# TensorE's order at the stage boundaries, a written order for the first norm, and GpSimd's work as written, in a two-layer hybrid decoder

## The chip, the cores and the metric

The kernel runs on one core of a Trainium2 chip. The metric is the device time of one launch in microseconds (us). The engines that matter are TensorE (PE in the profile: matrix products and transposes, results in the eight banks of PSUM), VectorE (DVE), ScalarE (ACT), GpSimd (POOL) and SyncE (SP, which only issues transfers). Each engine works through its own queue in order, and waits by semaphores for the others.

## What is computed

Two layers over 512 tokens of width 1024 in float32, each a half-weighted SwiGLU feed-forward, four token mixers between two projections, and a second feed-forward; a last norm ends it. Cut to what the change touches:

```python
D_MODEL = 1024; SEQ = 512; DEPTH = 2; D_FF = 2816

def rmsnorm(x, g):
    xf = x.astype(jnp.float32)
    y = xf * lax.rsqrt(jnp.mean(xf * xf, axis=-1, keepdims=True) + EPS)
    return (y * g.astype(jnp.float32)).astype(x.dtype)

def swiglu(h, w1, w3, w2):
    return (jax.nn.silu(h @ w1) * (h @ w3)) @ w2

for l in range(DEPTH):
    h = rmsnorm(x, ffn1_norm[l])
    x = x + FFN_RESIDUAL * swiglu(h, ffn1_w1[l], ffn1_w3[l], ffn1_w2[l])
    h = rmsnorm(x, mix_norm[l])
    p = h @ w_in[l]
...
    mix = jnp.concatenate([y_a, y_b, y_c, y_d], axis=-1)
    x = x + mix @ w_out[l]
    h = rmsnorm(x, ffn2_norm[l])
    x = x + FFN_RESIDUAL * swiglu(h, ffn2_w1[l], ffn2_w3[l], ffn2_w2[l])
return rmsnorm(x, final_norm)
```

## The kernel before

The 512 tokens are four blocks b = 0 to 3 of 128 (tiles `x0` to `x3`, rows are tokens). Every float32 operand of a product is split into a high part (a rounded copy, made by ScalarE as a cast) and a low part (the rest, made by VectorE as a subtraction), and each product is three TensorE passes: high by high, activation low by weight high, activation high by weight low (`mm3`, lines 107 to 109). In the feed-forwards the products follow a Strassen-like scheme on halves of the tokens: r = 1 are blocks 2 and 3, r = 0 are blocks 0 and 1.

The class `Norm` makes a normed operand in steps: `square` (ScalarE, one per half row, sums into `ss`), `root` (VectorE adds to `nv`, GpSimd raises to the power -1/2 into `ry`), `scale` (VectorE, `xn`), and `turn`: TensorE transposes the block into two banks `pt` (8 transposes of 128x128), ScalarE casts the high part (L210, or L189 for the mixers), VectorE subtracts the low part (L211, L190), and for the feed-forwards ScalarE also keeps plain copies (`B12f`, `B22f`, L214 and L215). `B12` and `B22` are the operands of blocks 2 and 3, `B11` and `B21` those of blocks 0 and 1; `third` makes one more operand, T3, from the plain copies.

There are four feed-forwards, named f0a, f0b, f1a, f1b (layer, then a for the one ahead of the mixers and b for the one behind), each `up` and then `down`; the mixers are L0 and L1, their norms m0 and m1. `up` begins with the last pair of columns without the scheme: 192 matmuls of 128x256, 96 for r = 1, then the transposes of blocks 0 and 1 (`turns`), then 96 for r = 0, all in the order of `mm3`. Its weights come in four quarters (m, k), each a transfer, a cast `whi` and a subtraction `wlo`. The mixers end with the output projection: eight banks `po` (block b, half c), to each of which `part(b, c)` adds 18 matmuls of 128x512 and, when the last mixer's result `ya` is there, the final loop 6 more; then VectorE adds the bank to x (L847), and the next norm begins.

TensorE's order is the written one (`manual_schedule` for PE). Inside `down` VectorE and ScalarE are also in written order; elsewhere a scheduler with priorities orders VectorE, ScalarE, GpSimd and the transfers. GpSimd also issues transfers that add to a tile (`accum_op`), lines 333, 336 and 393. The program opens with 40 matmuls on a constant (`WARM`), and the first norm, n0.

Of the kernel before, what the change touches and what calls it, by code (L numbers as in the profile page):

```python
# [42 lines left out]
C_ALL = C_R16 + 32  # L43
# [6 lines left out]
def trunk(ctx: ExitStack, tc: tile.TileContext, x, par, gains, tab, w13, w2, wi, wg, wo, out):  # L50
    nc = tc.nc
# [191 lines left out]

    HALF = (slice(0, 256), slice(256, 512))

    def up(f, nrm, turns, name):
        a = [
            [acts.tile([P, n, T], F32, tag=f"a{h}{j}", name=f"a{h}{j}_{name}") for j, (_, n) in enumerate(SUB)]  # L250
            for h in range(2)
# [13 lines left out]
        W = (P, 2, 4, P)

        def quarters(i):
            return {
                (m, k): load(w13[f, i, m, k], W, f"{name}{i}{m}{k}") for m in range(2) for k in range(2)
            }  # L270
# [313 lines left out]
    def mixers(l, nrm, nxt, turns):  # L584
# [89 lines left out]
        mix = {}  # L674
# [155 lines left out]
            mix[j] = split2(y, f"ya_{nm}{j}")  # L830


        wa = []
        for c in range(2):
            raw = load(wo[l, c, :, 6:8], (P, 2, T), f"{nm}oa{c}")
            wa.append(split_w(raw, (P, 2, T), f"{nm}oa{c}", acts, (f"q{2 * c}", f"q{2 * c + 1}")))
        part(0, 1)
        part(1, 1)
        for b in (2, 3, 0, 1):
            bs = slice(b * P, (b + 1) * P)  # L840
            for c in range(2):
                for e in range(2):
                    hi, lo = mix[e]
                    mm3(pw[b, c], hi[:, bs], lo[:, bs], wa[c][0][:, e], wa[c][1][:, e], False, e == 1)
                with tc.high_priority(offset=400):
                    xs = xt[b][:, c * T : (c + 1) * T]
                    V.tensor_tensor(xs, pw[b, c], xs, ALU.add)  # L847
                nxt.square(b, c)
            nxt.scale(b)
        for b in (2, 3):  # L850
            nxt.turn(b)


    ctx.enter_context(tc.manual_schedule(engines={mybir.EngineType.PE}))

    pd = bank("pd")
    for i in range(WARM):
        PE.matmul(pd[:, 0:P], mean_w, mean_w, start=True, stop=True)
    nrm = Norm("n0", 0)
    for b in (2, 3):  # L860
        for c in range(2):
            nrm.square(b, c)
        nrm.scale(b)
    for b in (0, 1):
        nc.sync.dma_start(xt[b], x[b])
# [4 lines left out]
    pt = const.tile([P, C_ALL], F32, name="pt")  # L870
    nc.sync.dma_start(pt, par)
    for b in (2, 3):
        nrm.turn(b)
    for l in range(DEPTH):

        def turns(nrm=nrm):
            for b in (0, 1):
                nrm.turn(b)

        nx = Norm(f"m{l}", 3 * l + 1)  # L880
        ffn(2 * l, nrm, nx, f"f{l}a", turns)
        nrm = nx

        def turns(nrm=nrm):
            for b in (0, 1):
# [12 lines left out]
        nrm = nx
# [84 lines left out]
```

## Time and profile before

| what | value |
|---|---|
| time, median of 3 runs | 1680.32 us (1679.66 to 1680.62) |
| the profiled execution's own time | 1681.03 us |
| its span, first to last instruction | 1679.3 us |
| PE busy | 98% of the span |
| DVE, ACT, POOL busy | 78%, 51%, 9% |
| mean granted TensorE clock | 0.993 |

TensorE is busy nearly all the time, so the table alone shows no room; what is to be read is where its few idle stretches lie, what ended each, and where the granted clock was 0.5. All times in rows are us from the start of the span, durations of single instructions in us.

### The profile page before, as it was taken

To read this page: it belongs to the slowest core of one execution; us is meant where nothing else is said; L and a number is where in the kernel's file an instruction comes from. 1 tells how busy PE (TensorE), PEld (TensorE's weight loads), DVE (VectorE), ACT (ScalarE), POOL (GpSimd) and SP (SyncE) were. 2 spreads that over 40 slices of the span, in tenths; PEclk is the share of its full clock that TensorE was granted. 3 is DMA by queue.
4 is the path that set the end of the run, shared out by engine and by line. 5 is a ranking of instruction groups with operands and counts; after the bars stand their busy time and mean duration, and the time that the engine had idled before them with its cause. 6 is when DMAs were issued, how large, how long until landed. Compare 5 with 4: busy or idle time off the path is not lost.

```text
span 1679.3 us, 27504 instructions
## 1 busy us (share of the span) xinstructions
PE 1645.1 (98%) x11072; PEld 1520.0 (91%) x11072; DVE 1307.3 (78%) x1661; ACT 850.0 (51%) x1238; POOL 145.5 (9%) x170
## 2 busy tenths in 40 slices
PE   8999999999998999999999999999999999999997
PEld 8999998888788999998899999988887799999886
DVE  5777778979856777788987777889796677777887
ACT  5454555553334555555655454556333445554654
POOL 1000002010010000101001000010000100000100
PEclk9999999999999999999999999999999999999999
DMA  6677669643331777779457777795333347777882
GB/s 203 189 182 182 177 195 242 190 157 101 113 87 63 183 185 182 191 204 263 151 132 184 187 182 184 200 270 182 119 90 97 90 113 178 186 180 185 234 229 101
DMA packets 80479, 283.94 MB, mean 169 GB/s; under 512 B 8928, under 2 KB 9056, under 8 KB 80352
## 3 DMA queue, kind: packets, MB, share of 16 engines
q1 hardware_dynamic: 61920, 217.18, 39.6%
q0 software_dynamic: 18432, 65.02, 22.3%
q8 instruction: 86, 1.41, 0.3%
q14 instruction: 41, 0.34, 0.1%
HBM read 280.07 MB, written 2.10 MB: 168 GB/s over the span
## 4 chain that ended last, share of the span: by engine, by line
PE 91%; DVE 5%; issue 1%; ACT 1%; POOL 1%; DMA 0%; POOLq 0%; DVEq 0%; ACTq 0%
PE px_f0b L107 3%; PE px_f1b L107 3%; PE px_f1a L107 3%; PE px_f1a L108 3%; PE px_f0a L108 3%; PE px_f0a L109 3%; PE px_f0b L109 3%; PE px_f1b L109 3%; PE px_f0a L107 3%; PE px_f1b L108 3%; PE px_f0b L108 3%; PE px_f1a L109 3%; PE pi_L L108 3%; PE pi_L L107 3%; PE pi_L L109 3%; PE pz_f1a L107 2%
## 5 line engine op out<-in xcount | busy, mean ns | idle before, releaser
L107 PE MATMUL pi_L<-gh_m,whi_L0i 128*128 128x512 f32 (+1 forms) x128 | 47.5, 371 | 0.3 <-ACT gh_m L189 0.3
L107 PE MATMUL pi_L<-gh_m,whi_L1i 128*128 128x512 f32 (+1 forms) x128 | 47.5, 371 | 0.3 <-ACT gh_m L189 0.3
L108 PE MATMUL pi_L<-gl_m,whi_L1i 128*128 128x512 f32 (+1 forms) x128 | 46.6, 364 | 0.6 <-DVE gl_m L190 0.6
L108 PE MATMUL pi_L<-gl_m,whi_L0i 128*128 128x512 f32 (+1 forms) x128 | 46.6, 364 | 0.6 <-DVE gl_m L190 0.6
L109 PE MATMUL pi_L<-gh_m,wlo_L0i 128*128 128x512 f32 (+1 forms) x128 | 46.4, 363 | 0.0
L109 PE MATMUL pi_L<-gh_m,wlo_L1i 128*128 128x512 f32 (+1 forms) x128 | 46.4, 363 | 0.0
L794 DVE SCALAR_TENSOR_TENSOR scr_gv_L<-scr_cv_L,pt,scr_gv_L 128x511 f32<-128x511 f32 (+29 forms) x60 | 43.8, 731 | 0.6
L794 DVE SCALAR_TENSOR_TENSOR scr_cv_L<-scr_cv_L,pt,scr_cv_L 128x511 f32<-128x511 f32 (+29 forms) x60 | 43.7, 728 | 0.1
L107 PEld LDWEIGHTS pi_L<-gh_m,whi_L0i 128*128 128x128 f32 x128 | 24.2, 189 | 4.9 <-ACT gh_m L189 0.6
L108 PEld LDWEIGHTS pi_L<-gl_m,whi_L1i 128*128 128x128 f32 x128 | 24.2, 189 | 4.8 <-DVE gl_m L190 0.8
L107 PEld LDWEIGHTS pi_L<-gh_m,whi_L1i 128*128 128x128 f32 x128 | 24.2, 189 | 4.8 <-ACT gh_m L189 0.6
L108 PEld LDWEIGHTS pi_L<-gl_m,whi_L0i 128*128 128x128 f32 x128 | 24.2, 189 | 4.8 <-DVE gl_m L190 0.8
L97 ACT CAST whi_L0i<-raw_L0i 128x1024 fp32r<-128x1024 f32 x14 | 14.6, 1051 | 27.4 <-PE pi_L L108 16.5
L97 ACT CAST whi_L1i<-raw_L1i 128x1024 fp32r<-128x1024 f32 x14 | 14.6, 1050 | 27.1 <-PE pi_L L108 16.2
L109 PEld LDWEIGHTS pi_L<-gh_m,wlo_L0i 128*128 128x128 f32 x128 | 24.2, 189 | 3.8
L109 PEld LDWEIGHTS pi_L<-gh_m,wlo_L1i 128*128 128x128 f32 x128 | 24.2, 189 | 3.8
L211 DVE TENSOR_TENSOR B_b<-pt_b,B_b 128x512 fp32r<-128x512 f32 x16 | 10.1, 681 | 19.7 <-ACT B_b L210 19.7
L108 PE MATMUL p_f0b<-B_b,whi_f0b 128*128 128x256 f32 x64 | 19.6, 307 | 2.8 <-DVE B_b L211 2.8
L108 PE MATMUL p_f1b<-B_b,whi_f1b 128*128 128x256 f32 x64 | 19.4, 304 | 2.8 <-DVE B_b L211 2.8
L107 PE MATMUL p_f0b<-B_b,whi_f0b 128*128 128x256 f32 x64 | 19.5, 305 | 2.2 <-ACT B_b L210 2.2
L107 PE MATMUL p_f1b<-B_b,whi_f1b 128*128 128x256 f32 x64 | 19.3, 302 | 2.2 <-ACT B_b L210 2.2
L107 PE MATMUL p_f0a<-B_n,whi_f0a 128*128 128x256 f32 x64 | 18.9, 295 | 2.1 <-ACT whi_f0a L278 1.8
(3407 smaller groups left out, 7281.5 us busy)
## 6 DMA issues: line engine op xcount, KB each, us to landing
raw_L0i<-wi SPq DMA_DIRECT2D x14, 512.0 KB, 3.7
raw_L1i<-wi SPq DMA_DIRECT2D x14, 512.0 KB, 3.7
tt_f0a<-w POOLq DMA_DIRECT2D x10, 512.0 KB, 8.5
tt_f0b<-w POOLq DMA_DIRECT2D x10, 512.0 KB, 8.6
tt_f1a<-w POOLq DMA_DIRECT2D x10, 512.0 KB, 8.7
tt_f1b<-w POOLq DMA_DIRECT2D x10, 512.0 KB, 8.3
gain<-gains SPq DMA_DIRECT2D x7, 512.0 KB, 4.5
raw_L0o<-wo SPq DMA_DIRECT2D x6, 512.0 KB, 3.8
```

The costliest lines, as they stand in the source:

```text
L97: S.copy(hi, raw)
L107: PE.matmul(ps, sh, mh, start=first, stop=False, skip_group_check=more)
L108: PE.matmul(ps, sh, ml, start=False, stop=False, skip_group_check=more)
L109: PE.matmul(ps, sl, mh, start=False, stop=last, skip_group_check=more)
L211: V.tensor_tensor(lo[:, :, s], ps[q], hi[:, :, s].bitcast(F32), ALU.subtract)
L794: V.scalar_tensor_tensor(acc[:, kk:], v[:, : T - kk], cw, acc[:, kk:], ALU.mult, ALU.add)
```

## The change

Six things change. (1) At the start 24 constant matmuls stand in place of 40, with 3 more behind each of the first two transposed blocks; the first norm's VectorE, ScalarE and SP work is in written order, in which blocks 2 and 3 are finished before blocks 0 and 1, and two of the first weight quarters are fetched ahead of `x0` and `x1`. (2) The 192 opening matmuls of `up` go by part: for each r and m all high by high (16), then all activation low (16), then all weight low (16). (3) `turns`, the transposes of blocks 0 and 1, stand 32 matmuls earlier, inside r = 1, and `third` ahead of r = 1. (4) In the mixers `turns` stands one group of 24 matmuls earlier. (5) At the end of the mixers blocks 2 and 3 are finished ahead of `part(1, 1)`, and their transposes stand between the last groups of blocks 0 and 1; the last two weight tiles share two buffers (q0, q1) in place of four (q0 to q3). (6) GpSimd's instructions stand in written order.

```diff
-WARM = 40
+WARM = 24
...
         ps = {(m, e): bank(f"p{2 * e + 1}_{name}{i}{m}") for m in range(2) for e in range(2)}
+        nrm.third()
+
         for r in (1, 0):
             for m in range(2):
-                for e in range(2):
-                    for k in range(KD):
-                        hi, lo = w[m, k // 4]
-                        g = nrm.op[f"B{k // 4 + 1}{r + 1}"]
-                        mm3(
-                            ps[m, e][:, HALF[r]], hi[:, e, k % 4], lo[:, e, k % 4],
-                            g[0][:, k % 4], g[1][:, k % 4], k == 0, k == KD - 1,
-                        )
-            if r == 1:
-                nrm.third()
-                turns()
+                for n, (x, y) in enumerate(((0, 0), (0, 1), (1, 0))):
+                    if (r, m, n) == (1, 1, 1):
+                        turns()
+                    for e in range(2):
+                        for k in range(KD):
+                            PE.matmul(
+                                ps[m, e][:, HALF[r]], w[m, k // 4][x][:, e, k % 4],
+                                nrm.op[f"B{k // 4 + 1}{r + 1}"][y][:, k % 4],
+                                start=n == 0 and k == 0, stop=n == 2 and k == KD - 1,
+                            )
...
         proj_mm(pg, wgate, HALF[1])
+        turns()
         proj_mm(pv, wval, HALF[1])
-        turns()
...
-            wa.append(split_w(raw, (P, 2, T), f"{nm}oa{c}", acts, (f"q{2 * c}", f"q{2 * c + 1}")))
+            S.copy(wah[:, c], raw)
+            V.tensor_tensor(wal[:, c], raw, wah[:, c].bitcast(F32), ALU.subtract)
+
+        def ending(b, c):
+            bs = slice(b * P, (b + 1) * P)
+            for e in range(2):
+                hi, lo = mix[e]
+                mm3(pw[b, c], hi[:, bs], lo[:, bs], wah[:, c, e], wal[:, c, e], False, e == 1)
+            with tc.high_priority(offset=400):
+                xs = xt[b][:, c * T : (c + 1) * T]
+                V.tensor_tensor(xs, pw[b, c], xs, ALU.add)
+            nxt.square(b, c)
+
         part(0, 1)
+        for b in (2, 3):
+            ending(b, 0)
+            ending(b, 1)
+            nxt.scale(b)
         part(1, 1)
-        for b in (2, 3, 0, 1):
...
+        for b in (0, 1):
+            ending(b, 0)
+            nxt.turn(2 + b)
+            ending(b, 1)
+            nxt.scale(b)
+
+
+    ctx.enter_context(tc.manual_schedule(engines={mybir.EngineType.PE, mybir.EngineType.Pool}))
...
+    with tc.manual_schedule(
+        engines={mybir.EngineType.DVE, mybir.EngineType.Activation, mybir.EngineType.SP}
+    ):
+        for k in range(2):
+            raw[0, k] = quarter_of(0, KH - 1, 0, k, "f0a")
+        for b in (0, 1):
+            nc.sync.dma_start(xt[b], x[b])
+        for k in range(2):
+            raw[1, k] = quarter_of(0, KH - 1, 1, k, "f0a")
+        pt = const.tile([P, C_ALL], F32, name="pt")
+        nc.sync.dma_start(pt, par)
+        warm_up(WARM)
+        for b in (2, 3):
             for c in range(2):
+                nrm.square(b, c)
+            nrm.scale(b)
...
         for b in (2, 3):
+            nrm.turn(b)
+            warm_up(3)
```

Where this moves instructions is seen at three places. At the start, ScalarE's queue before had all eight squares (`sq`, block and half in the name) and then the casts of blocks 2 and 3 ahead of the first weight:

```order
L136 ACTIVATE sq_n031_151,ss_n03_148<-x3_84 128x512
L136 ACTIVATE sq_n000_162,ss_n00_161<-x0_81 128x512
...
L136 ACTIVATE sq_n011_175,ss_n01_172<-x1_82 128x512
L210 CAST B12_n0_185<-pt_n020_189 128x4x128
L210 CAST B22_n0_186<-pt_n021_196 128x4x128
L210 CAST B12_n0_185<-pt_n030_205 128x4x128
L210 CAST B22_n0_186<-pt_n031_212 128x4x128
L278 CAST whi_f0a1000_241<-raw_f0a1000_233 128x1024
L278 CAST whi_f0a1001_245<-raw_f0a1001_235 128x1024
L214 COPY B12f_n0_187<-pt_n020_189 128x4x128
```

and now has, from the last square of block 3 on:

```order
L136 ACTIVATE sq_n031_149,ss_n03_146<-x3_84 128x512
L277 CAST whi_f0a1000_234<-raw_f0a1000_99 128x1024
L210 CAST B12_n0_157<-pt_n020_161 128x4x128
L210 CAST B22_n0_158<-pt_n021_168 128x4x128
L277 CAST whi_f0a1001_238<-raw_f0a1001_101 128x1024
L214 COPY B12f_n0_159<-pt_n020_161 128x4x128
L136 ACTIVATE sq_n000_201,ss_n00_200<-x0_81 128x512
L215 COPY B22f_n0_160<-pt_n021_168 128x4x128
L210 CAST B12_n0_157<-pt_n030_180 128x4x128
L136 ACTIVATE sq_n001_203,ss_n00_200<-x0_81 128x512
L210 CAST B22_n0_158<-pt_n031_187 128x4x128
L136 ACTIVATE sq_n010_212,ss_n01_211<-x1_82 128x512
```

The weight casts moved ahead of squares and copies, and block 3's two casts behind block 0's squares. At the end of the mixers of layer 0, TensorE's queue before was: the last group of block 1, all transposes of blocks 2 and 3 (`pt_b02`, `pt_b03`), and then the three passes of `up` in turn:

```order
L109 MATMUL po_L011_4800<-whi_L0oa1_4777,scr_ya_L01h_4766 128x512
L163 MATMUL pt_b020_4925<-ident_89,xn_b02_4844 128x128 x4
L163 MATMUL pt_b021_4932<-ident_89,xn_b02_4844 128x128 x4
L163 MATMUL pt_b030_4941<-ident_89,xn_b03_4869 128x128 x4
L163 MATMUL pt_b031_4948<-ident_89,xn_b03_4869 128x128 x4
L107 MATMUL p1_f0b100_4993<-B12_b0_4921,whi_f0b1000_4977 128x256
L108 MATMUL p1_f0b100_4993<-B12_b0_4921,whi_f0b1000_4977 128x256
L109 MATMUL p1_f0b100_4993<-B12_b0_4921,wlo_f0b1000_4979 128x256
```

and now block 3's transposes have a group of block 1 behind them, and `up` opens with high parts alone:

```order
L163 MATMUL pt_b030_4917<-ident_89,xn_b03_4841 128x128 x4
L163 MATMUL pt_b031_4924<-ident_89,xn_b03_4841 128x128 x4
L107 MATMUL po_L011_4843<-oah_L0_4762,scr_ya_L00h_4752 128x512
...
L109 MATMUL po_L011_4843<-oah_L0_4762,scr_ya_L01h_4759 128x512
L291 MATMUL p1_f0b100_4984<-B12_b0_4872,whi_f0b1000_4968 128x256 x4
L291 MATMUL p1_f0b100_4984<-B22_b0_4873,whi_f0b1001_4972 128x256 x4
L291 MATMUL p3_f0b100_4985<-B12_b0_4872,whi_f0b1000_4968 128x256 x4
L291 MATMUL p3_f0b100_4985<-B22_b0_4873,whi_f0b1001_4972 128x256 x4
```

On VectorE the same place before had block 3's low parts at the end, directly behind each other:

```order
L148 TENSOR_SCALAR nv_b01_4915<-ss_b01_4903 128x1
L211 TENSOR_TENSOR B12_b0_4921<-pt_b020_4925,B12_b0_4921 128x4x128
L156 SCALAR_TENSOR_TENSOR xn_b01_4919<-x1_82,ry_b01_4917,gain2_4838 128x1024
L211 TENSOR_TENSOR B12_b0_4921<-pt_b030_4941,B12_b0_4921 128x4x128
L211 TENSOR_TENSOR B22_b0_4922<-pt_b021_4932,B22_b0_4922 128x4x128
L211 TENSOR_TENSOR B22_b0_4922<-pt_b031_4948,B22_b0_4922 128x4x128
```

and now has a weight's low part (L279), three adds to x and a `scale` (L156) between them:

```order
L211 TENSOR_TENSOR B22_b0_4873<-pt_b021_4883,B22_b0_4873 128x4x128
L847 TENSOR_TENSOR x0_81<-po_L001_4772,x0_81 128x512
L279 TENSOR_TENSOR wlo_f0b1010_4978<-raw_f0b1010_4964,whi_f0b1010_4976 128x1024
L148 TENSOR_SCALAR nv_b00_4901<-ss_b00_4869 128x1
L847 TENSOR_TENSOR x1_82<-po_L010_4651,x1_82 128x512
L156 SCALAR_TENSOR_TENSOR xn_b00_4905<-x0_81,ry_b00_4903,gain2_4810 128x1024
L211 TENSOR_TENSOR B12_b0_4872<-pt_b030_4917,B12_b0_4872 128x4x128
L847 TENSOR_TENSOR x1_82<-po_L011_4843,x1_82 128x512
L211 TENSOR_TENSOR B22_b0_4873<-pt_b031_4924,B22_b0_4873 128x4x128
```

Block 2's low parts moved ahead, and block 3's behind work for blocks 0 and 1. On GpSimd four powers `ry` of the second feed-forward's norm now stand ahead of its first two adding transfers, and the mixers' mask behind the powers of their norm.

## Rows read from the trace of the kernel before

**Rows 1.** List of TensorE's waits: waited for, us in total, times, longest.
```profile
PE p_f0b L108 <- DVE B_b L211: 2.8, 2, 2.3
...
PE pi_L L108 <- DVE gl_m L190: 1.1, 2, 0.6
...
PE p_f1a L108 <- DVE B_a L211: 0.6, 1, 0.6
```

**Rows 2.** Busy time by stretch: stretch, length, five engines (instructions), granted clock, DMA.
```profile
19.03:22.45 3.42, 3.08 (x14) 3.08 (x15) 3.42 (x4) 1.56 (x3) 0.00 (x0) 0.50 0.64 164
...
507.14:513.97 6.83, 6.04 (x28) 6.04 (x29) 4.38 (x6) 2.81 (x4) 0.00 (x0) 0.50 0.22 77
1333.16:1339.99 6.83, 5.24 (x24) 5.24 (x25) 5.07 (x6) 3.13 (x5) 0.00 (x0) 0.50 0.22 77
```

**Rows 3.** Timeline of TensorE, start and f0a: start, us, instruction, idle before.
```profile
1.13 11.21 PE L858 MATMUL pd<-mean_w 128*128 128x128 f32 x80 [1.13 <-DVE expo L66]
...
19.37 0.58 PE L109 MATMUL p_f0a<-B_n,wlo_f0a 128*128 128x256 f32 x1 [1.94 <-DVE wlo_f0a L280]
...
31.85 0.28 PE L108 MATMUL p_f0a<-B_n,whi_f0a 128*128 128x256 f32 x1
31.97 0.28 PE L109 MATMUL p_f0a<-B_n,wlo_f0a 128*128 128x256 f32 x1
32.09 1.91 PE L163 MATMUL pt_n<-ident,xn_n 128*128 128x128 f32 x16
...
35.51 0.28 PE L109 MATMUL p_f0a<-B_n,wlo_f0a 128*128 128x256 f32 x1
```

**Rows 4.** Timeline of TensorE, end of mixers L0 and opening of f0b.
```profile
482.45 0.39 PE L107 MATMUL po_L<-whi_L0o,scr_yc_L00h 128*128 128x512 f32 x1
...
501.50 1.91 PE L163 MATMUL pt_b<-ident,xn_b 128*128 128x128 f32 x16
505.25 0.39 PE L107 MATMUL p_f0b<-B_b,whi_f0b 128*128 128x256 f32 x1 [1.84 <-ACT B_b L210]
507.93 0.58 PE L108 MATMUL p_f0b<-B_b,whi_f0b 128*128 128x256 f32 x1 [2.29 <-DVE B_b L211]
...
514.03 0.28 PE L109 MATMUL p_f0b<-B_b,wlo_f0b 128*128 128x256 f32 x1
```

**Rows 5.** Timeline of VectorE (first row) and ScalarE, start.
```profile
7.94 2.48 DVE L156 SCALAR_TENSOR_TENSOR xn_n<-x,ry_n,gain 128x1024 f32<-128x1024 f32 x2
...
9.17 0.63 ACT L136 ACTIVATE sq_n<-x 128x512 f32<-128x512 f32 x1 [1.58 <-DMA x<-x]
...
10.68 0.63 ACT L136 ACTIVATE sq_n<-x 128x512 f32<-128x512 f32 x1
...
16.62 1.10 ACT L214 COPY B12f_n<-pt_n 128x512 f32<-128x512 f32 x2
17.58 1.10 ACT L278 CAST whi_f0a<-raw_f0a 128x1024 fp32r<-128x1024 f32 x1
```

**Rows 6.** SP's timeline, then the second of these two issues: KB, us to landing.
```profile
2.19 0.99 SPq L865 DMA_DIRECT2D x<-x  x2
...
x<-x SPq DMA_DIRECT2D x1, 512.0 KB, 7.8
```

**Rows 7.** Timeline, end of mixers L0: VectorE, GpSimd.
```profile
483.26 0.69 DVE L713 TENSOR_TENSOR scr_ya_L01h<-scr_cv_L,scr_ya_L01h 128x512 fp32r<-128x512 f32 x1
...
507.19 1.88 DVE L211 TENSOR_TENSOR B_b<-pt_b,B_b 128x512 fp32r<-128x512 f32 x3
...
503.26 0.55 POOL L114 TENSOR_TENSOR ry_b<-nv_b,expo 128x1 f32<-128x1 f32 x1 [3.12 <-DVE nv_b L148]
```

**Rows 8.** Timeline, opening of f1a: TensorE, GpSimd.
```profile
846.67 0.28 PE L107 MATMUL p_f1a<-B_a,whi_f1a 128*128 128x256 f32 x1
...
848.95 0.39 PE L109 MATMUL p_f1a<-B_a,wlo_f1a 128*128 128x256 f32 x1 [0.44 <-DVE wlo_f1a L280]
...
854.28 1.40 POOL L114 TENSOR_TENSOR ry_a<-nv_a,expo 128x1 f32<-128x1 f32 x1 [1.59 <-DVE nv_a L148]
```

More of the change, by code (lines that the diff above doesn't have):

```diff
@@ L244, in trunk, with quarter_of, up @@
     HALF = (slice(0, 256), slice(256, 512))
-    def up(f, nrm, turns, name):
+    W = (P, 2, 4, P)
+    def quarter_of(f, i, m, k, name):
+        return load(w13[f, i, m, k], W, f"{name}{i}{m}{k}")
+    def up(f, nrm, turns, name, raw=None):
         a = [
@@ L263, in sums @@
             V.tensor_tensor(a21, a11, a21, ALU.subtract)
[L265 to L270, printed above, removed]
         i = KH - 1
-        raw = quarters(i)
+        if raw is None:
+            raw = {(m, k): quarter_of(f, i, m, k, name) for m in range(2) for k in range(2)}
         w = {}
@@ L557, in down, with ffn @@
                     nxt.scale(t)
-    def ffn(f, nrm, nxt, name, turns, end=False):
-        down(f, *up(f, nrm, turns, name), nxt, name, end)
+    def ffn(f, nrm, nxt, name, turns, end=False, raw=None):
+        down(f, *up(f, nrm, turns, name, raw), nxt, name, end)
     class Scratch:
@@ L830, in mixers @@
             mix[j] = split2(y, f"ya_{nm}{j}")
-        wa = []
+        wah, wal = (acts.tile([P, 2, 2, T], F32R, tag=f"q{e}", name=f"oa{'hl'[e]}_{nm}") for e in range(2))
         for c in range(2):
             raw = load(wo[l, c, :, 6:8], (P, 2, T), f"{nm}oa{c}")
-            wa.append(split_w(raw, (P, 2, T), f"{nm}oa{c}", acts, (f"q{2 * c}", f"q{2 * c + 1}")))
+            S.copy(wah[:, c], raw)
[9 more added lines that the diff above has]
+            nxt.square(b, c)
@@ L837, in mixers @@
         part(0, 1)
+        for b in (2, 3):
+            ending(b, 0)
+            ending(b, 1)
+            nxt.scale(b)
         part(1, 1)
-        for b in (2, 3, 0, 1):
-            bs = slice(b * P, (b + 1) * P)
-            for c in range(2):
[L842 to L849, printed above, removed]
@@ L850, in mixers @@
-        for b in (2, 3):
[L851 to L865, printed above, removed]
+        for b in (0, 1):
[3 more added lines that the diff above has]
+            nxt.scale(b)
@@ new lines, in trunk, with warm_up @@
+    ctx.enter_context(tc.manual_schedule(engines={mybir.EngineType.PE, mybir.EngineType.Pool}))
+    pd = bank("pd")
+    def warm_up(n):
+        for _ in range(n):
+            PE.matmul(pd[:, 0:P], mean_w, mean_w, start=True, stop=True)
+    nrm = Norm("n0", 0)
+    raw = {}
+    with tc.manual_schedule(
[11 more added lines that the diff above has]
+        for b in (2, 3):
+            for c in range(2):
+                nrm.square(b, c)
+            nrm.scale(b)
+        for b in (2, 3):
+            nrm.turn(b)
+            warm_up(3)
@@ L869, in trunk @@
         nrm.scale(b)
[L870 to L873, printed above, removed]
     for l in range(DEPTH):
@@ L880, in trunk @@
         nx = Norm(f"m{l}", 3 * l + 1)
-        ffn(2 * l, nrm, nx, f"f{l}a", turns)
+        ffn(2 * l, nrm, nx, f"f{l}a", turns, raw=raw)
+        raw = None
         nrm = nx
```

## The prediction

> **What bounds the kernel now.** TensorE: it is busy 98% of the span, so an edit pays only where TensorE stands idle or runs at half clock. I read the list of its waits first, then the granted clock by stretch, then the timeline of TensorE at each place the list names, and last the engines it waits for. The list names places where one stage hands over to the next: the openings of `up`, the transposes of blocks 0 and 1, the mixers' first projections [rows 1]. [...] Inside the long loops of `up` and `down` nothing is named, so nothing there is counted.
>
> Two paces are needed. At full clock a 128x256 matmul starts 0.12 behind the last (31.85, 31.97 [rows 3]); a transpose too (16 in 1.91). At half clock 14 start in 3.08, about 0.213 each [rows 2].
>
> **The transposes of blocks 0 and 1 (edits 3 and 4).** In f0a 16 transposes begin at 32.09; unhindered the third matmul behind them would start 1.79 + 3 x 0.12 later, at about 34.2. It starts at 35.51 [rows 3]: 1.35 lost, waiting for the casts and then the low parts of what was just transposed. The same wait stands in the list for f0b (2.8 in two waits of which one is 2.3), f1a (0.6) and twice for the mixers (1.1 in two) [rows 1]; f1b has the same code. Now 32 matmuls of 128x256 in `up` (3.8 us), or 24 in the mixers (2.9), lie between transposes and use. The chain to be hidden ends 1.35 late, so both cover it: 5 places (f0a is counted below) x 1.35 = 6.8 gained. The bound from the other side: with the transposes 32 matmuls earlier the normed blocks 0 and 1 must be ready earlier. In f1a TensorE now gets there at 846.67 + 64 x 0.12 = 854.35 [rows 8], while block 1's power ended at 854.28 + 1.40 = 855.7 and the `scale` needs 1.24 more [rows 5, 8]. In the new order the first power no longer stands behind an adding transfer and T3's subtraction stands behind block 0's `scale`, which I put at 1.3 earlier for the whole chain: ready at about 855.6, while block 0's 8 transposes last until 855.3. So 0.4 is lost there (none to 2).
>
> **The opening of f1a (edit 2).** TensorE waits 0.44 for `wlo`, and a lone matmul in a stopped stream costs 0.26 more (0.38 in place of 0.12) [rows 8]. The low weights are now used 32 matmuls (3.8 us) later: 0.7 gained.
>
> **The end of the mixers (edits 2 and 5), f0b and f1b.** In f0b the transposes begin at 501.50; unhindered the 30th matmul of `up` would start 1.79 + 29 x 0.12 later, at 506.8. It starts at 514.03 (28 of them within the half-clock stretch) [rows 2, 4]: 7.3 lost, some 4.8 by the two waits and 2.5 by the clock. In f1b the clock came back 0.8 earlier in the program (1339.99 against 513.97 + 826.82, the distance of the two places), so 6.9.
>
> What is late next? Take the new order with durations of before: adds to x and low parts of a transposed half block 0.63 [rows 7], a `scale` 1.24, a square 0.76, a copy or cast of a half block 0.55, a cast or low part of a weight 1.1 to 1.2 [rows 5], a power 0.55 [rows 7], a group of six 128x512 matmuls 1.36 (0.227 each: 18 from 482.45 take 4.08 [rows 4]). Three checks:
> First, the endings now begin behind `part(0, 1)`, 4.08 after 482.45, at 486.5; `ya` is complete at 483.26 + 0.69 = 483.95 [rows 4, 7], so 2.6 of slack are left of the 6.6 that were there.
> Second, block 3 must be scaled when its transposes come up, at 501.2 (486.5, four groups 5.4, `part(1, 1)` 4.1, three groups and a block of transposes 5.1). Its second square stands behind a weight cast that waits for `part(1, 1)`; I get 498.0. Slack 3.
> Third, `up` opens at 503.6 with 16 high matmuls and needs block 3's casts then (503.1 and 503.6, just in time), and block 3's low parts at 505.6 and 506.1. VectorE has in its queue, from 499.2 on: add, two low parts, add, a weight's low part, `nv`, add, `scale` (with a power ahead), low part, add, low part: 505.7 for the first, 506.95 for the second. So TensorE waits about 0.1 and then 0.85, and 0.25 to start again: 1.2, with 0.2 for one more change between transposes and matmuls 1.4 (0 if VectorE keeps up; 3 if a power or a cast is late). Nothing there leaves TensorE idle as long as the 1.84 and 2.29 of before, so the clock should stay up. Gained: 7.3 + 6.9 - 2 x 1.4 = 11.4.
>
> **The start (edit 1).** `x2`, `x3` and the gain keep their places in SP's queue, so the first `scale` still starts at 7.94 [rows 5]. The new order puts block 3's `nv` behind it: second `scale` 10.1 to 11.4. Warm-up matmuls end at about 8.6 (48 of the 80 passes; the first 20 run at 0.21, by the time of before [rows 3]), block 2's transposes follow at 9.3, block 3's at 11.4 to 12.3, the last warm-ups end at 13.0. The first weight quarter takes `x0`'s place and lands at 9.1, which is when the square waiting for `x0` starts [rows 5]; the second takes `x1`'s, 2.67 + 7.8 = 10.4 [rows 6]; `x0` and `x1` come 1.3 apart behind, 11.7 and 13.0. ScalarE then runs, from 9.15: weight cast, two casts, weight cast, copy, square, copy, cast (ends 14.9), square, cast (ends 16.1). TensorE starts four matmuls at 14.9 and streams from 16.2. The other 92 of r = 1 take 11.0 and the transposes inside them 1.9, and low parts and the other weights come in time (`wlo` 1 and 2 by 15.1, casts 3 and 4 by 20.6 against 21.3). So r = 0 begins at 29.1 and its third matmul starts at 29.4, against 35.51 [rows 3]: 6.1 gained, if the clock stays up.
>
> **GpSimd as written (edit 6).** The adding transfers of f0b and f1b issue some 13 us later, behind the last power; their result is first needed in the third product of the loop, behind all 192 opening matmuls (23 us): nothing. The mixers' mask stands behind powers and is needed in the gating, far later: nothing.
>
> **Sum.** 6.8 - 0.4 + 0.7 + 11.4 + 6.1 = 24.6. Against the profiled execution, 1681.03 (span 1679.3 and 1.7 around it), that is 1656.4. The runs' median is 0.7 below the profiled execution, so **1656**.
>
> [...] The rows show the clock falling in f0b behind idle stretches of 1.84 and 2.29 with a lone matmul between [rows 2, 4]. [...]
>
> **Rivals.**
> B, the start falls to half clock: between 13.0 and 16.2 TensorE has four matmuls to do, much as between 505.25 and 507.93. For: the lone matmul of f0b did not keep the clock up. Against: four are more than one, warm-ups run until 13.0, and idle stretches are 1.9 and 0.8. One stretch of 3.4 at half clock does 16 matmuls in place of 28: 1.5 lost; two, 3. Time about 1658.
> C, VectorE is later than I have it at the mixers' end: TensorE's wait for block 3's low parts reaches 2 to 3 and the clock falls again. It decides from about 2 of waiting. 1.5 more waiting and 2 of clock at each end: 1663.
> D, the other side: the order by parts loads new weights for every matmul, where before two in three followed a matmul with the same ones. If that set the pace at 0.213, 768 matmuls cost 0.09 more each: 1656 + 71 = 1727; it decides against the change from 0.032 a matmul. Against it: L109 follows L108 with other weights at 0.12 [rows 3].
> E, the change doesn't do what it says: the opening of `up` is faster but the first products of the loop then wait for VectorE's and ScalarE's splits, which follow the transposes by some 10 us. For: VectorE is 78% busy. Against: those splits also start earlier, with the transposes. Half given back: 1668.
>
> **Chances.** The forecast as summed 0.60, B 0.17, C 0.13, E 0.06, D 0.02, other 0.02. The low end takes all residues at zero (2.8 and 0.4) and a start faster by 1: 1651.5; the high end takes C and a little: 1664. A change under 0.2% (3.4 us) is about what a measurement can't tell from none. Faster by more than that needs all but D, most of E's worst and the unknown: 0.95; within 0.02; slower 0.03.
>
> **What would show it.** Right: no 0.50 stretch near the ends of the mixers; TensorE's waits for `gl_m` and at L211 behind blocks 0 and 1 gone; a wait of about 0.9 for block 3's low part at the opening of f0b and f1b; the first matmul of `up` near 14.9 and, in f0a, the loop's first product near 40.6 (29.1 and 96 x 0.12). Wrong: a half-clock stretch at 15 to 19 (B) or at the mixers' end (C), a spacing over 0.12 within `up` (D), waits at the first products of the loop (E).

## The result and the profile after

The changed kernel takes **1654.53 us** (median of 4 runs, 1654.36 to 1656.20) against 1680.47 for the kernel before, run beside it: a ratio of 0.9848, 95% interval 0.9831 to 0.9865, 25.9 gained. The forecast was 1656, range 1651.5 to 1664. The profiled execution took 1654.36, span 1652.6, 26.7 shorter than before.

TensorE's waits, after (answers to [rows 1]):

```profile
PE pt_m L163 <- DVE xn_m L156: 2.3, 2, 1.2
PE p_f0a L291 <- ACT B_n L210: 1.4, 2, 1.1
...
PE p_f1b L291 <- DVE B_b L211: 0.5, 1, 0.5
PE p_f0b L291 <- DVE B_b L211: 0.5, 1, 0.5
```

The rows with `gl_m`, with L211 behind blocks 0 and 1 and with `wlo_f0a` and `wlo_f1a` are gone, and f0b and f1b wait 0.5 for low parts in place of 2.8. To put the gain at its places, I read where the same instruction stands in both timelines of TensorE: the first transposes for m0, for f1a (`pt_a`) and for m1 (L163) and, in each layer's mixers, the first product with the mixer result `yd` (L107). A count below 16 only means that the view ends inside the row. Before:

```profile
350.44 1.74 PE L163 MATMUL pt_m<-ident,xn_m 128*128 128x128 f32 x11 [1.13 <-DVE xn_m L156]
...
456.88 0.50 PE L107 MATMUL po_L<-whi_L0o,scr_yd_L00h 128*128 128x512 f32 x1 [0.81 <-ACT scr_yd_L00h L711]
...
840.42 1.85 PE L163 MATMUL pt_a<-ident,xn_a 128*128 128x128 f32 x12 [1.13 <-DVE xn_a L156]
1177.24 1.96 PE L163 MATMUL pt_m<-ident,xn_m 128*128 128x128 f32 x13 [1.13 <-DVE xn_m L156]
...
1283.69 0.50 PE L107 MATMUL po_L<-whi_L1o,scr_yd_L10h 128*128 128x512 f32 x1 [0.82 <-ACT scr_yd_L10h L711]
```

After, with the rows of the start and of f0b that answer to [rows 3, 4]:

```profile
13.95 0.74 PE L291 MATMUL p_f0a<-B_n,whi_f0a 128*128 128x256 f32 x4 [1.09 <-ACT B_n L210]
15.05 3.62 PE L291 MATMUL p_f0a<-B_n,whi_f0a 128*128 128x256 f32 x28 [0.36 <-ACT B_n L210]
18.51 2.08 PE L291 MATMUL p_f0a<-B_n,wlo_f0a 128*128 128x256 f32 x16
...
343.13 2.29 PE L163 MATMUL pt_m<-ident,xn_m 128*128 128x128 f32 x16 [1.16 <-DVE xn_m L156]
...
448.16 0.50 PE L107 MATMUL po_L<-whi_L0o,scr_yd_L00h 128*128 128x512 f32 x1 [0.83 <-ACT scr_yd_L00h L711]
...
494.58 2.88 PE L291 MATMUL p_f0b<-B_b,whi_f0b 128*128 128x256 f32 x20
497.92 1.70 PE L291 MATMUL p_f0b<-B_b,whi_f0b 128*128 128x256 f32 x12 [0.46 <-DVE B_b L211]
...
824.15 2.29 PE L163 MATMUL pt_a<-ident,xn_a 128*128 128x128 f32 x16 [1.16 <-DVE xn_a L156]
1159.28 2.29 PE L163 MATMUL pt_m<-ident,xn_m 128*128 128x128 f32 x16 [1.17 <-DVE xn_m L156]
...
1264.33 0.50 PE L107 MATMUL po_L<-whi_L1o,scr_yd_L10h 128*128 128x512 f32 x1 [0.83 <-ACT scr_yd_L10h L711]
```

How far a row moved, less how far the row ahead of it moved, is what the stretch between gained (the last one from the spans):

| stretch | forecast | measured |
|---|---|---|
| start and f0a | 6.1 | 350.44 - 343.13 = 7.3 |
| turns in mixers L0, L1 | 1.35, 1.35 | 1.4, 1.4 |
| end of L0 and f0b | 7.3 - 1.4 + 1.35 = 7.25 | 16.27 - 8.72 = 7.55 |
| f1a | 1.35 - 0.4 + 0.7 = 1.65 | 17.96 - 16.27 = 1.7 |
| end of L1 and f1b | 6.9 - 1.4 + 1.35 = 6.85 | 26.7 - 19.36 = 7.3 |
| sum | 24.6 | 26.7 |

The 16 matmuls from 18.51 take 2.08, a start every 0.12: the order by parts, where every matmul loads other weights, costs nothing (rival D). The three stretches at 0.50 of [rows 2], each at or right behind a hand-over, are gone. By stretch (columns as there), at the start and in f0b:

```profile
13.95:17.35 3.40, 3.04 (x23) 2.84 (x24) 3.33 (x7) 3.40 (x10) 0.55 (x1) 1.00 0.13 40
...
494.20:497.60 3.40, 3.19 (x23) 2.70 (x21) 3.27 (x5) 1.93 (x5) 0.55 (x1) 1.00 0.50 154
497.60:501.00 3.40, 3.08 (x25) 3.08 (x26) 2.42 (x4) 0.96 (x3) 2.37 (x3) 1.00 0.13 11
```

### The profile page after: what moved, and what is told of

Read it like the earlier page. It is cut to its first block, busy times and chain, and to the rows that moved or that the text cites. A ratio compares the mean times of both kernels' runs of the same rounds, so it can differ in the third digit from the quotient of the medians.

```text
span 1652.6 us, 27463 instructions
## 1 busy us (share of the span) xinstructions
PE 1633.3 (99%) x11052; PEld 1510.3 (91%) x11052; DVE 1309.0 (79%) x1661; ACT 849.8 (51%) x1238; POOL 146.5 (9%) x170
## 4 chain that ended last, share of the span: by engine, by line
PE 92%; DVE 4%; ACT 1%; issue 1%; POOL 1%; DMA 0%; SPq 0%; POOLq 0%; DVEq 0%; ACTq 0%
PE px_f0b L107 3%; PE px_f1b L107 3%; PE px_f0a L107 3%; PE px_f1a L107 3%; PE px_f1a L108 3%; PE px_f0b L108 3%; PE px_f1b L109 3%; PE px_f0a L109 3%; PE px_f0b L109 3%; PE px_f0a L108 3%; PE px_f1b L108 3%; PE px_f1a L109 3%; PE pi_L L107 3%; PE pi_L L108 3%; PE pi_L L109 3%; PE pz_f0b L109 2%
## 5 line engine op out<-in xcount | busy, mean ns | idle before, releaser
L107 PE MATMUL pi_L<-gh_m,whi_L1i 128*128 128x512 f32 (+1 forms) x128 | 47.4, 371 | 0.0
L107 PE MATMUL pi_L<-gh_m,whi_L0i 128*128 128x512 f32 (+1 forms) x128 | 47.4, 371 | 0.0
L108 PE MATMUL pi_L<-gl_m,whi_L1i 128*128 128x512 f32 (+1 forms) x128 | 46.5, 363 | 0.0
L108 PE MATMUL pi_L<-gl_m,whi_L0i 128*128 128x512 f32 (+1 forms) x128 | 46.5, 363 | 0.0
L107 PEld LDWEIGHTS pi_L<-gh_m,whi_L0i 128*128 128x128 f32 x128 | 24.2, 189 | 4.3 <-issue 0.5
L107 PEld LDWEIGHTS pi_L<-gh_m,whi_L1i 128*128 128x128 f32 x128 | 24.2, 189 | 4.3 <-issue 0.5
L108 PEld LDWEIGHTS pi_L<-gl_m,whi_L0i 128*128 128x128 f32 x128 | 24.2, 189 | 4.1 <-issue 0.5
L108 PEld LDWEIGHTS pi_L<-gl_m,whi_L1i 128*128 128x128 f32 x128 | 24.2, 189 | 4.1 <-issue 0.5
L99 DVE TENSOR_TENSOR wlo_L1i<-raw_L1i,whi_L1i 128x1024 fp32r<-128x1024 f32 x14 | 17.0, 1218 | 4.0 <-ACT whi_L1i L97 4.0
L99 DVE TENSOR_TENSOR wlo_L0i<-raw_L0i,whi_L0i 128x1024 fp32r<-128x1024 f32 x14 | 17.1, 1218 | 4.0 <-ACT whi_L0i L97 4.0
L114 POOL TENSOR_TENSOR ry_m<-nv_m,expo 128x1 f32<-128x1 f32 x8 | 9.2, 1155 | 119.3 <-DVE nv_m L148 116.6
L847 DVE TENSOR_TENSOR x<-po_L,x 128x512 f32<-128x512 f32 x16 | 11.0, 685 | 10.9 <-PE po_L L109 10.9
L114 POOL TENSOR_TENSOR ry_a<-nv_a,expo 128x1 f32<-128x1 f32 x8 | 8.4, 1048 | 119.0 <-DVE nv_a L148 119.0
L136 ACT ACTIVATE sq_a<-x 128x512 f32<-128x512 f32 x16 | 10.1, 632 | 16.2 <-DVE x L486 16.0
```

Of the source, the lines that this page charges most:

```text
L99: V.tensor_tensor(lo, raw, hi.bitcast(F32), ALU.subtract)
L114: G.tensor_tensor(y, v, expo[:, 0:n], ALU.pow)
L136: S.activation(sq, xt[b][:, c * T : (c + 1) * T], AF.Square, scale=1.0 / 32.0, accum_out=self.ss[b][:, c : c + 1],)
```

## The experiments

Times are medians, with the range of the runs in brackets; a kernel's difference is to 1654.5 where nothing else is said.

**One edit undone at a time.** First the order by parts (edit 2):

```diff
-                for n, (x, y) in enumerate(((0, 0), (0, 1), (1, 0))):
...
+                for e in range(2):
+                    for k in range(KD):
+                        if (r, m, e, k) == (1, 1, 0, 5):
+                            turns()
...
+                        mm3(
```

> The changed kernel, but the opening of up goes again matmul by matmul through the three passes (edit 2 undone); the transposes of blocks 0 and 1 keep their place, 33 matmuls ahead of their use. Theory (a hand-over costs what TensorE waits, and the order by part hides the low parts): at f0b and f1b the first matmul starts as in the changed kernel (494.6) and the second waits for block 3's low part, there at 496.7: 1.7 idle in place of 0.46, 1.3 more at each. f1a waits for wlo again, 0.7. At the start the second matmul waits for a low part until 15.1, and the third weight's low part comes late: 1.0. Sum 4.3: 1658.8, clock at 2.4 GHz throughout, because no idle stretch reaches 1.84 and 2.29 in a row as before. Rival 1, clock: 1.7 of idle with a lone matmul ahead is enough for the clock to fall, at each end about 2 more: 1663. Rival 2: the order by part adds nothing, all comes from the moves: 1654.5 to 1655.

It took 1660.5 (1659.5 to 1662.0), so 6.0 were lost. TensorE at the start and in f0b, then the stretches at the lower clock at the start, in f0b and in f1b:

```profile
14.18 0.38 PE L107 MATMUL p_f0a<-B_n,whi_f0a 128*128 128x256 f32 x1 [1.08 <-ACT B_n L210]
15.40 0.57 PE L108 MATMUL p_f0a<-B_n,whi_f0a 128*128 128x256 f32 x1 [0.84 <-DVE B_n L211]
...
498.94 0.39 PE L108 MATMUL p_f0b<-B_b,whi_f0b 128*128 128x256 f32 x1 [1.87 <-DVE B_b L211]
...
15.45:18.86 3.41, 3.41 (x16) 3.41 (x17) 3.16 (x5) 3.41 (x8) 1.78 (x2) 0.50 0.02 5
500.14:503.56 3.42, 3.42 (x19) 3.42 (x18) 2.51 (x3) 0.63 (x3) 2.39 (x3) 0.50 0.17 12
1319.34:1322.76 3.42, 3.42 (x18) 3.42 (x18) 2.56 (x3) 0.46 (x2) 2.39 (x3) 0.50 0.25 29
```

The second matmul of f0b waits 1.87, near the theory's 1.7, but the clock falls behind that (rival 1). In f1b it is the same, and at the start the clock falls behind waits of 1.08 and 0.84.

Second, I undid the order at the mixers' end (edit 5, with its two weight buffers kept):

```diff
-        for b in (2, 3):
-            ending(b, 0)
-            ending(b, 1)
-            nxt.scale(b)
         part(1, 1)
-        for b in (0, 1):
-            ending(b, 0)
-            nxt.turn(2 + b)
-            ending(b, 1)
-            nxt.scale(b)
+        for b in (2, 3, 0, 1):
+            ending(b, 0)
+            ending(b, 1)
+            nxt.scale(b)
+        for b in (2, 3):
+            nxt.turn(b)
```

> The changed kernel, but the end of the mixers has the order of before: part(0,1), part(1,1), the endings of blocks 2, 3, 0, 1, then the transposes of blocks 2 and 3 (edit 5's order undone, its two weight buffers kept). Theory: the casts end 1.84 behind the transposes as before; the 16 high matmuls cover most of the 2.29 that the low parts took, 0.75 of it stays. Lost 2.6 and twice 0.25 for a new start, 3.1 in place of 0.7 at each of two ends: 1654.5 + 4.8 = 1659.3, with the clock up (one idle stretch of 1.84, then 16 matmuls). Rival 1, clock: it falls as before, 2 to 2.5 more at each end: 1663.3 to 1664.3. Rival 2: the order by part alone was what counted, and the moved blocks change nothing: 1655.

It took 1660.4 (1659.1 to 1660.8), so 5.9 were lost: theory and rival 1 are each half right. The waits were 1.79 and 0.24 in f0b, 1.80 and 0.24 in f1b, and only in f0b did the clock fall. TensorE, then by stretch, f0b and f1b:

```profile
496.28 0.74 PE L291 MATMUL p_f0b<-B_b,whi_f0b 128*128 128x256 f32 x4 [1.79 <-ACT B_b L210]
...
1316.26 0.74 PE L291 MATMUL p_f1b<-B_b,whi_f1b 128*128 128x256 f32 x4 [1.80 <-ACT B_b L210]
1317.23 2.44 PE L291 MATMUL p_f1b<-B_b,whi_f1b 128*128 128x256 f32 x16 [0.24 <-ACT B_b L210]
...
497.28:500.69 3.41, 3.41 (x16) 3.41 (x17) 2.81 (x4) 2.14 (x4) 1.69 (x2) 0.50 0.57 74
1317.23:1320.64 3.41, 2.95 (x20) 2.54 (x21) 2.84 (x4) 2.14 (x4) 1.71 (x2) 1.00 0.61 82
```

Third, I put the transposes of blocks 0 and 1 back (edits 3 and 4):

```diff
-                    if (r, m, n) == (1, 1, 1):
-                        turns()
...
+            if r == 1:
+                turns()
...
-        turns()
         proj_mm(pv, wval, HALF[1])
+        turns()
```

> The changed kernel, but the transposes of blocks 0 and 1 stand right ahead of their use again, in up (between r = 1 and r = 0) and in the mixers (behind the last group of 24) (edits 3 and 4 undone, third kept ahead of r = 1). Theory: in the mixers 1.41 each comes back, as the traces of before and after differ there. In up only the cast's wait comes back, 0.34 and 0.25 to start again, 0.6 at each of four, since the 16 high matmuls cover the low parts: 2.8 + 2.4 = 5.2, so 1659.7. Rival 1, the prediction's own term: 1.35 at each of the six places, 8.1, so 1662.6. Rival 2: the order by part already hides it in up: 1657.3.

It took 1659.65 (1659.3 to 1660.1), so 5.1 were lost: the theory's 5.2. In `up` only the casts' wait of 0.34 comes back at each place.

Fourth, I undid the start (edit 1): `WARM = 40`, no constant matmuls between the transposes, no written order, `x0` and `x1` ahead of the weights.

> The changed kernel with the start of before: 40 constant matmuls, no more between the transposes, order of the first norm left to the scheduler, x0 and x1 ahead of the weights (edit 1 undone alone). Theory: ScalarE's queue is that of before, so the first matmul starts at 15.9 and the stream at 16.8 in place of 15.05; with the order by part neither the low part of the operand nor wlo is waited for: 1.75 lost, 1656.3, no half clock. That would mean that of the 7.3 which f0a gained only 1.75 is the written order's and 4.2 the order by part's. Rival 1 (the prediction as written, which put 6.1 down to edit 1): 1660.5. Rival 2, clock: the 1.8 of idle at 14 brings 3.4 or 6.8 at half clock: 1657.8 to 1659.3.

It took 1656.1 (1655.6 to 1656.7), so 1.6 were lost. TensorE waits 1.77 for the first cast of a weight and 0.21 for the second, and the clock stays up (0.999 in the mean; 20 matmuls from 17.57 take 2.65, a start every 0.12):

```profile
16.62 0.74 PE L291 MATMUL p_f0a<-B_n,whi_f0a 128*128 128x256 f32 x4 [1.77 <-ACT whi_f0a L277]
```

Fifth, I left GpSimd's order to the scheduler (edit 6):

```diff
-    ctx.enter_context(tc.manual_schedule(engines={mybir.EngineType.PE, mybir.EngineType.Pool}))
+    ctx.enter_context(tc.manual_schedule(engines={mybir.EngineType.PE}))
```

> The changed kernel with GpSimd's order left to the scheduler (edit 6 undone alone). Theory (the prediction's): nothing, 1654.5 within 0.5; the adding transfers of f0b and f1b issue some 13 earlier again and nobody waits for them. Rival: in f1a the first power stands behind an adding transfer again, block 0 comes 0.7 later to its transposes, which now stand 32 matmuls earlier, and TensorE waits 0.5 to 2 there: 1655 to 1656.5.

It took 1655.9 (1655.5 to 1656.2), so 1.4 were lost: the rival came. TensorE, then GpSimd, in f1a of e4_pool_free:

```profile
838.50 1.03 PE L163 MATMUL pt_a<-ident,xn_a 128*128 128x128 f32 x8
840.95 1.09 PE L163 MATMUL pt_a<-ident,xn_a 128*128 128x128 f32 x8 [1.42 <-DVE xn_a L156]
...
834.89 0.89 POOL L333 DMA_DIRECT2D raw_f1a0d<-w  x1 [11.42 <-DVE nv_a L148]
835.50 1.09 POOL L114 TENSOR_TENSOR ry_a<-nv_a,expo 128x1 f32<-128x1 f32 x1
838.18 1.40 POOL L114 TENSOR_TENSOR ry_a<-nv_a,expo 128x1 f32<-128x1 f32 x1 [1.59 <-DVE nv_a L148]
```

A transfer issue stands ahead of block 0's power again, block 1's power begins 1.6 later than in the changed kernel (838.18 against 836.55), and TensorE stops for 1.42 ahead of block 1's transposes.

**One edit alone.** The kernel before with nothing but the order by parts:

> The kernel before, with the order by part in the opening of up as its only change (edit 2 alone; transposes, end of the mixers, start and GpSimd as before). Theory (local terms, with overlaps): the start gains what the changed kernel with the old start had of it, 4.2; behind the transposes of blocks 0 and 1 only the cast's wait stays, 0.75 gained at four places, 3.0; at f0b and f1b the mixers' end in the old order lost 3.6 a place in place of 7.3, so 7.2; wlo in f1a 0.7. Sum 15.1: 1665.4. Rival 1 (the terms of the prediction, each edit with its own): edit 2 alone gives only wlo's 0.7, 1680. Rival 2, clock: it falls once or twice more at f0b and f1b because the wait for the casts is whole, 1.8 for each 3.4 at half clock: 1667 to 1669.

It took 1666.9 (1666.3 to 1667.4), against 1680.8 for the kernel before, run beside it: 13.9 gained of 15.1 expected. The clock fell in f0b and f1b once each (3.4 at 0.50) behind waits of 2.13 and 1.85. Undone, the edit costs 6.0; alone, it brings 13.9: the edits hide the same waits. The five undone singly cost 20.0 together, 6 less than they bring. In all five, `third` stayed ahead of r = 1 and the last two weight tiles kept their two buffers, so what these two are worth is not shown.

**The clock.** The trace counts two passes for each constant matmul (80 for 40 [rows 3]), so the changed kernel has 48 passes at its start and 12 behind the first two transposed blocks. Here two are left, and none behind the transposes (`WARM = 1`, `warm_up(3)` removed):

> The changed kernel with 2 constant passes at the start in place of 48 and none behind the first two transposed blocks (part of edit 1 undone). Theory: ScalarE's queue sets when the stream may start; TensorE itself comes to the first transposes at half clock: 8 transposes take 1.7 to 1.9 in place of 1.0, so the casts of block 3 come 0.8 later, and the stream runs at 1.2 GHz for one or two stretches of 3.4 us, 1.7 lost in each: 1657 to 1658.7. Rival 1: the warm-up does nothing for the path (the clock comes up as soon as the stream runs): 1655.3. [...]

It took 1658.05 (1657.7 to 1658.4), so 3.5 were lost. By stretch, e6_no_warm:

```profile
15.90:19.30 3.40, 3.40 (x15) 3.24 (x15) 3.33 (x5) 2.86 (x6) 0.55 (x1) 1.00 0.00 0
...
22.70:26.10 3.40, 3.40 (x31) 3.40 (x30) 1.45 (x2) 1.05 (x1) 0.00 (x0) 1.00 1.02 408
```

The first matmul of `up` starts at 15.90 in place of 13.95, and the first stretch runs at the slow pace (15 matmuls in 3.4). In the changed kernel 32 matmuls had started by 18.51, here by 22.24. The constant passes are worth 3.5.

And e1_mm3_order with its waits of 0.84, 1.87 and 1.87 filled by work that is thrown away:

```diff
+                        if (r, m, e, k) == (1, 0, 0, 0):
+                            for _ in range({"f0a": 9, "f1a": 0}.get(name, 15)):
+                                PE.matmul(
+                                    ps[m, e][:, HALF[r]], hi[:, e, k], g[0][:, k], start=True, stop=True
+                                )
                         mm3(
```

> The kernel e1_mm3_order, with the first matmul of up done 15 times more in f0b and f1b and 9 times more in f0a, each time starting its sum anew, so that TensorE works through the waits of 1.87, 1.87 and 0.84 without getting further (the work is thrown away). Theory (of the 6.0 that e1 lost, 4.5 was the clock: three stretches of 3.4 at 1.2 GHz, 12 matmuls of 0.12 lost in each): the waits stay filled, the half clock goes, 1660.5 - 4.5 = 1656.0, or 0.5 less where a lone matmul's restart also goes. Rival (the loss is the wait itself, or the lower clock only goes with it by chance): 1660.5, or 0.3 more for matmuls that end behind the wait.

It took 1657.5 (1657.4 to 1658.0): 3.1 less than e1_mm3_order by the medians, and 4.55 by the two profiled executions (1661.96 and 1657.41). The two ran on different chips; the kernel before took 1680.6 beside the one and 1681.6 beside the other. The runs of e1_mm3_order lie between 1659.5 and 1662.0, with mean clocks of 0.998 to 0.996: it seems that the clock does not fall at all three places in each. The three stretches at 0.50 of e1_mm3_order are gone in h1_filled. At the start and in f0b (f1b reads 1.00 too):

```profile
13.78:17.20 3.42, 3.42 (x28) 3.42 (x29) 3.35 (x7) 3.42 (x10) 0.55 (x1) 1.00 0.17 59
497.02:500.44 3.42, 3.35 (x28) 3.14 (x27) 2.44 (x5) 1.78 (x4) 1.17 (x2) 1.00 0.15 60
```

So TensorE's idle time made the clock fall, and thirty-nine useless matmuls make that kernel faster.

**What is left.** First, block 3's low parts ahead of the scales of blocks 0 and 1:

```diff
-            nxt.turn(2 + b)
+            with tc.high_priority(offset=2000):
+                nxt.turn(2 + b)
             ending(b, 1)
+        for b in (0, 1):
             nxt.scale(b)
```

> The changed kernel with block 3's two low parts ahead of the scales of blocks 0 and 1 in VectorE's queue at the end of the mixers. Theory: the 0.46 that TensorE still waits in f0b and f1b, and 0.25 for the new start, go: 2 x 0.7 = 1.4, so 1653.1; the powers of blocks 0 and 1 come 1.3 later, still ahead of their transposes 64 matmuls on. Rival 1: the later scales are now late for those transposes, and the wait only moves: 1654.5. Rival 2, within the noise of the first kernels: 1654.

It took 1653.0 (1652.0 to 1653.6): 1.5 gained, and the waits of 0.46 are gone. Then the start, with the plain copies moved out of `turn`:

```diff
         for b in (2, 3):
-            nrm.turn(b)
+            nrm.turn(b, False)
             warm_up(3)
+        for b in (2, 3):
+            nrm.copies(b)
```

> The changed kernel with the four plain copies of blocks 2 and 3 behind both blocks' casts in ScalarE's queue at the start, so block 3's casts stand directly behind the second weight cast and one square. Theory: ScalarE sets the start; block 3's casts end at 12.4 and 13.5 in place of 13.9 and 15.0, TensorE starts at 12.9 and streams from 13.5: 1.5 to 1.6 gained, 1652.9, if block 3's low parts and the third weight's cast (18.1 against 18.7) keep up. Rival 1: the stream meets VectorE, whose low part of the second weight now stands behind a power's add, and waits 0.5 to 1: 1653.7. Rival 2: the clock falls at the start because fewer passes stand ahead of the stream: 1656.

It took 1653.45 (1652.5 to 1654.6): 1.1 gained of 1.6 expected. TensorE streams from 13.70 in place of 15.05, but the profiled execution waits 1.15 at the end of `up` in f0b. There VectorE's addition that frees a bank stands behind a sum of weights that waits for a transfer (`raw_f0bb`). The sum starts at 717.19, and in the changed kernel at 717.20: TensorE came earlier, the transfer did not. Such a wait stands in the profiles of six of the twelve experiments (0.26 to 1.15) and not in that of the changed kernel; two of the six, e2_end_order and e3_turns_back, are slower than it, so an earlier TensorE is not the only reason, and the other was not looked for. Both together:

> The changed kernel with both reorderings that were measured one at a time: block 3's low parts ahead of the scales at the mixers' end, and the plain copies behind the casts at the start. Theory: they are 490 apart and add: 1654.5 - 1.5 - 1.3 = 1651.7, give or take 0.7 for the transfer that in some executions lands late at the end of up in f0b or f1b (0.4 to 1.15). Rival: TensorE now reaches that transfer earlier in every execution, and one of the two gains is given back there: 1653.

It took 1651.6 (1650.5 to 1653.0): the two gains add, within the spread. Last, with both, the wait of 1.16 that stands ahead of three transposes (`pt_m` twice, `pt_a`), by an edit in `down`:

```diff
-            if not end:
-                for t in range(2):
-                    nxt.turn(2 + t)
             for t in range(2):
                 for s in (tail, tail + 1):
                     product(s, (t,))
+                    if not end and (s, t) == (tail, 0):
+                        for b in (2, 3):
+                            nxt.turn(b)
```

> As f9_both, and in three of the four down stages the transposes of blocks 2 and 3 stand behind the first group of the last products in place of ahead of all of them, so that the scale they wait for (1.16 three times) lies beside 1.4 of matmuls. Theory: 3 x 1.2 = 3.5 gained over f9_both, 1648.2; the transposes still end 2.7 ahead of the next stage's opening, and casts and low parts need 1.4 to 2.4 of that. Rival 1: the low parts come late for the mixers' or f1a's opening and 0.5 to 1 goes back at each of three: 1650.5. Rival 2: the last but one product's low weight, split behind the second scale, is late, and the wait only moves: 1651.7.

It took 1648.3 (1647.3 to 1649.2), 3.3 less than f9_both, a ratio to before of 0.9808 (0.9793 to 0.9822): the fastest of these kernels. TensorE's waits, f10_three, with the three of 1.16 gone:

```profile
PE pz_f1b L108 <- DVE wlo_f1bg L464: 1.4, 1, 1.4
...
PE px_f0b L107 <- DVE s_f0b L368: 0.7, 1, 0.7
PE px_f1b L107 <- DVE s_f1b L368: 0.5, 1, 0.5
PE p_f1a L297 <- ACT whi_f1a L283: 0.3, 1, 0.3
```

## Why the prediction was right

The sum came out because it counts what TensorE loses at each place, and all edits were in. How the prediction split it among the edits failed in part, as the terms show.

**Transposes of blocks 0 and 1.** The term was 1.35 a place; in the mixers 1.4 was measured. In `up` the term is right as a sum, but e3_turns_back shows that the move itself earns only about 0.6 a place there (5.1 less twice 1.4, over four places); the order by parts earns the rest.

**f1a.** A loss of 0.4 was forecast. The list of waits has none there, but there is no slack either: block 1's `scale` ends at 839.26 (837.98 + 1.28), when block 0's transposes end, and the 16 transposes take 2.09 in place of 1.91, so about 0.2 was lost:

```profile
838.32 2.09 PE L163 MATMUL pt_a<-ident,xn_a 128*128 128x128 f32 x16
```

But I had priced GpSimd's written order at nothing, for f0b, f1b and the mask alone. The 1.3 that I let the f1a chain gain is that edit's, and e4_pool_free puts 1.4 on it.

**End of the mixers.** Block 3's second low part was forecast for 3.35 behind the opening of `up` (506.95 - 503.6); it ended at 497.87 (497.19 and 0.68 on VectorE), 3.3 behind 494.58. Twenty matmuls would have taken 2.4 to the one that needs it; it started 3.34 behind the first, and 0.1 went at the new start: 1.0 lost in place of 1.4, which is the 0.3 to 0.45 that each end gained beyond the forecast. The clock stayed up.

**The start.** It gained 1.2 more than forecast. The first matmul stood at 13.95, not 14.9, the loop's first product at 39.45, not 40.6. The step that was mis-sized is ScalarE's queue: I added whole durations, but the next instruction starts 0.95 behind a cast of 1.06 and 0.48 behind a copy of 0.60. That is about 0.7 of the first matmul's 0.95; the other 0.3 is that the first weight's cast began at 8.87, not 9.15:

```profile
10.77 1.06 ACT L277 CAST whi_f0a<-raw_f0a 128x1024 fp32r<-128x1024 f32 x1
11.72 0.60 ACT L214 COPY B12f_n<-pt_n 128x512 f32<-128x512 f32 x1
12.20 0.65 ACT L136 ACTIVATE sq_n<-x 128x512 f32<-128x512 f32 x1
```

And I put the 6.1 down to edit 1. With that edit undone the prediction's terms would give 1660.6 (1654.5 + 6.1); 1656.1 was measured. The order by parts alone (g1_parts_only) brings 4.7 of the 7.3, since m0's first transposes stand 4.7 earlier than before (350.44) there:

```profile
345.75 2.29 PE L163 MATMUL pt_m<-ident,xn_m 128*128 128x128 f32 x16 [1.16 <-DVE xn_m L156]
```

Low parts and `wlo` are waited for no longer, and the half clock of [rows 2] at the start does not come.

**The rivals.** B (half clock at the start), C (VectorE late and the clock down), D (0.21 a matmul) and E (waits at the loop's first products) did not come. D's count of weights was wrong besides: before, only one matmul in three (L108, behind L107) followed one with the same weights, not two. As for C, 0.46 left the clock up, and 1.79 or more brought it down at five of the six openings of f0b and f1b in e1_mm3_order, e2_end_order and g1_parts_only. But 1.80 and 0.24 in f1b of e2_end_order left it up, as did 1.77 and 0.21 at the start of e5_start_back and g1_parts_only, while 1.08 and 0.84 at the start of e1_mm3_order brought it down. So the length of the waits alone does not decide, and what else does is open.

**Idle time and the clock.** At five of those six openings the clock fell behind gaps of 1.79 to 2.13, and at the start of e1_mm3_order behind 1.08 and 0.84 with one matmul between. With the waits of e1_mm3_order filled (h1_filled) its three stretches at 0.50 did not come: idle time was the cause. As for fewer constant passes, 60 in place of 80 kept the pace at the start (28 matmuls from 15.05 take 3.62), and 2 did not (15 in 3.4 from 15.90, e6_no_warm). The 1.2 and 2.4 GHz of the expectations are shown by no run: the views give a granted clock of 0.50 and 1.00, and a 128x256 matmul started every 0.213 (16 in 3.41, e1_mm3_order) and every 0.12.

## What to carry to other kernels

Where a product is split into passes, order the opening of a stage so that the operand made last is used last: that one loop alone brought 13.9 of 26. Where TensorE waits 1 to 2 us at the opening of a stage, read the granted clock behind the wait: here a stretch of 3.4 at 0.50 did 16 matmuls (e1_mm3_order) in place of 28 (h1_filled), which cost about 1.5 at 0.12 each. Several edits can hide the same wait, so undo each alone, and try it alone, before saying what it is worth. Sum an engine's queue by start-to-start distances, not by durations, and price a queue's new order at every place where another engine waits for it.

## What the hardware showed that I had not expected

GpSimd's power of 128x1 took 0.55. Where it began while VectorE added or subtracted two tiles in SBUF, it ended 0.4 behind VectorE and so took longer: 1.02 to 1.48 beside one such instruction in before, after and e4_pool_free, and 2.13 beside two in a row (339.63 in after). In f1a, after, VectorE and then GpSimd:

```profile
836.32 1.22 DVE L225 TENSOR_TENSOR T3f_a<-B22f_a,B12f_a 128x1024 f32<-128x1024 f32 x1
...
836.55 1.40 POOL L114 TENSOR_TENSOR ry_a<-nv_a,expo 128x1 f32<-128x1 f32 x1 [1.59 <-DVE nv_a L148]
```

Beside a VectorE instruction that reads a PSUM bank it took 0.55 (834.41 in after, with an addition to `x` from 834.18). VectorE took longer in its turn: in the mixers, after, a `scale` that begins 0.07 behind GpSimd's mask takes 1.64; in before, where the mask stands at 342.45, the same `scale` takes 1.28 (361.64). Not every pair shows it: in before, a `scale` at 7.94, 0.02 behind a power, takes its 1.28. The mask and the `scale`:

```profile
354.26 0.64 POOL L597 TENSOR_SCALAR_AFFINE_SELECT scr_tab_L<-scr_tab_L 128x512 f32<-128x512 f32 x1
...
354.33 1.64 DVE L156 SCALAR_TENSOR_TENSOR xn_m<-x,ry_m,gain 128x1024 f32<-128x1024 f32 x1 [0.44 <-POOL ry_m L114]
```

So GpSimd's written order cost VectorE 0.36 there, though no wait of TensorE in the list comes from it.

At the program's start the granted clock reads 1.00 while the first 20 constant passes of before take 4.25, 0.21 each, and the first 15 matmuls of `up` in e6_no_warm 3.4, 0.23 each. Elsewhere that pace reads 0.50 (16 in 3.41, e1_mm3_order), so there I went by the pace, not by the column.
